# A two-block transformer in split fp32: first pair behind a norm in plain form, the two weight rings moved within a 256-byte line, and constant parts computed in other stages

## The chip, the cores and the metric

The kernel runs on one core of one Trainium2 chip. The metric is the device time of one execution in microseconds (us). The kernel before takes 1993.64 us, the median of three runs (1984.35 to 1995.71). Names of engines as in the profile: PE is TensorE's matmul, PEld its weight load, DVE is VectorE, ACT is ScalarE, POOL is GpSimd, SP is SyncE, whose queue issues the weight loads.

## The reference, cut to what matters

512 tokens of width 1024 go through two transformer layers, all in fp32. The second layer gets scales and shifts from a conditioning vector `c`. Cut to what the change touches:

```python
def second_block(x, c, w_ada, b_ada, ...):
    sh1, sc1, gt1, sh2, sc2, gt2, sh3, sc3, gt3 = split(silu(c) @ w_ada + b_ada, 9)
    u = rmsnorm_2(h, g_ff1) * (1 + sc1) + sh1
    h = h + 0.5 * gt1 * ((silu(u @ w1_gate) * (u @ w1_up)) @ w1_down)    # width 2816
    u = rmsnorm_2(h, g_mix) * (1 + sc2) + sh2
    ...                              # u @ w_in, differential attention, mLSTM
    h = h + gt2 * (merged @ w_out)
    u = rmsnorm_2(h, g_ff2) * (1 + sc3) + sh3
    h = h + 0.5 * gt3 * ((silu(u @ w2_gate) * (u @ w2_up)) @ w2_down)
    return rmsnorm_2(h, g_final)
```

Ahead of it, `first_block` does gated linear attention and windowed attention, and a feed-forward part of width 4096 with a squared relu; its output is normed once more and is then `h`.

## The kernel before, in words

**Precision.** Each fp32 operand is split into a high and a low part (`split`, L115 to L118: ACT writes the high part, DVE the difference). A product of two tiles is three matmuls: low by high, high by low, high by high (`mm3`, L124 to L126; `mm3k`, L130 to L132). Activations lie as 8 tiles of 128 features by 512 tokens, one per k.

**Plain and saving products.** `gemm` gives one output tile of 128 features by 512 tokens: 8 k times 3 = 24 matmuls of 512 columns. The wide matrices of the feed-forward parts go through `w_group` (L509) instead: a group makes four output tiles with the seven-product scheme of Strassen and Winograd, each product (`w_prod`, L498) 24 matmuls of 256 columns. It needs sums of the four weight blocks (L535, L543, L544, L554, on DVE), sums of the activation quarters (`w_sums`, L504 to L507), and DVE work behind the products (L527, L551, L558).

**Stages.** Attention of layer 1, its output product, feed-forward 1 (8 groups, each followed by 8 `down` tiles of the group before), the first feed-forward of layer 2 (`ffn_w(1, ...)`), the mixers, `merged`, `w_out2`, and the second feed-forward (`ffn_w(2, ...)`). Between the pieces of a group `fill` puts `down` tiles, `ada_step` (a piece of `silu(c) @ w_ada`, a 512 KB load and one DVE instruction of 1.28 us) and, in `ffn_w(1)`, `gate_weights`.

**A norm's border.** The scale of the norm comes only when all 8 tiles of the residual `res` stand. So four output tiles of the coming stage are computed ahead from the unscaled tiles (`pr` in the profile, 96 matmuls): the scale is multiplied in later (`ahead`), and the shift's part, weight times shift, is a constant per output feature. `prebias` (L415) computes that constant: load of the weight tile, one multiplication and seven multiply-adds on DVE (L423, L425, tile `pa`), a matmul of one column (L427), a copy (L428). Before, these calls stand in the loop over the 8 residual tiles just ahead of each border. Behind the border, `modulate` (L587) makes the scaled tiles one after the other, together with the sums that `w_group` wants, and ten groups follow.

**Order.** A list scheduler arranges the instructions of all engines when the kernel is built; each engine then works in order. Weight tiles go through rings of buffers: `wp` has three each of `raw`, `wh` and `wl`, the pool of a feed-forward stage (`hp`, tiles `s_...`) two of `wh` and `wl`. Before, a counter sends two of five splits to the second ring (L473, L474).

**Places in memory.** `shift` allocates a few bytes so that what follows starts elsewhere. As built before, the weight tiles of both rings start at byte 224 of a 256-byte line, and the activation tiles `uh`, `ul`, `vh`, `vl`, `hh`, `hl` at byte 160.

Of the kernel before, what the change touches and what calls it, by code (L numbers as in the profile page):

```python
# [18 lines left out]
P = 128  # L19
T = 512  # L20
# [34 lines left out]
class Kern:  # L55
    def __init__(self, tc, I, O, ctx):
        self.tc, self.nc, self.I, self.O = tc, tc.nc, I, O
        self.ctx = ctx
        ep = ctx.enter_context
        self.cst = ep(tc.tile_pool(name="cst", bufs=1))  # L60
        self.wp = ep(tc.tile_pool(name="wp", bufs=3))
        self.shift(self.wp, 128)
        self.sm = ep(tc.tile_pool(name="sm", bufs=2))
        self.wk = ep(tc.tile_pool(name="wk", bufs=2))
        self.dr = ep(tc.tile_pool(name="dr", bufs=1, space=bass.MemoryType.DRAM))
        self.roles = None
# [107 lines left out]

    def gemm(self, name, i, xh, xl, nk=KT, order=None, w=None):
        wh, wl = w or self.wtile(name, i, nk)
        ps = self.mmps()
        self.mm3(ps, wh, wl, xh, xl, nk, order)
        return ps
# [48 lines left out]
    def block1(self):  # L228
# [55 lines left out]
        def down(c, h, m2):  # L284
            w = self.w_split(self.w_load(I["w_ffd"][4 * c + m2]))
            wh, wl = (t.rearrange("p (a k m) -> p a k m", a=2, k=4) for t in w)
            for a in range(2):
                m = 2 * m2 + a
                ps = self.mmps()
                for k in range(4):  # L290
                    self.mm3k(ps, wh[:, a, k], wl[:, a, k], h[0][:, k // 2, k % 2], h[1][:, k // 2, k % 2], k, 3)
                V.tensor_tensor(out=res[:, m], in0=ps, in1=res[:, m], op=ALU.add)
                if c == NG_FF - 1:
                    if m == 0:
                        self.ada_gain(0)
                    self.boundary_tile(m)
                yield

        queue = iter(())
        for g in range(NG_FF):  # L300
            h = hid()

            def evict(c, a, b):
                s = slice(c * HT, (c + 1) * HT)
                for i, x in enumerate((a, b)):
                    r = self.wk.tile([P, T], F32, name="r1", tag="e1") if c and not i else x
                    rv = r.rearrange("p (a c) -> p a c", a=2)
                    V.scalar_tensor_tensor(out=rv, in0=x.rearrange("p (a c) -> p a c", a=2), scalar=0.0, in1=R[:, s].unsqueeze(1).to_broadcast([P, 2, HT]),
                                           op0=ALU.max, op1=ALU.mult)
                    act(out=r, in_=r, func=AF.Square)  # L310
                    self.split(h[0][:, :, i, s], h[1][:, :, i, s], rv)

            def fill(j):
                for _ in range(FILL_FF[g][j]):
                    next(queue)
                self.ada_step(j < 3)

            self.w_group(I["w_ffw"][g], (vh, vl), tt, ready, evict, fill, g == 0)
            assert next(queue, None) is None or g == 0
            queue = itertools.chain(*[down(g, h, m2) for m2 in range(KT // 2)])  # L320
# [6 lines left out]
    def ada_start(self, pool):  # L327
        nc = self.nc
        self.adp = pool
        if not hasattr(self, "mods"):  # L330
            self.mods = self.cst.tile([P, 72], F32, name="mods")
            self.sh, self.G = [None] * 3, [None] * 3
# [21 lines left out]
    def ada_gain(self, i):  # L354
# [3 lines left out]
        assert self.ada_i >= 24 * i + 16  # L358
        self.sh[i] = mod(3 * i)
        g = self.G[i] = c.tile([P, KT], F32, name=f"G{i}")  # L360
# [13 lines left out]
    def second_set(self):  # L374
        up = self.ue.enter_context(self.tc.tile_pool(name="up", bufs=1))
        self.shift(up, 64)
        return tuple(up.tile([P, KT, T], F32R, name=n) for n in ("vh", "vl"))


    def boundary_tile(self, m):  # L380
# [88 lines left out]

    def w_tile(self, tag, dt, own=None):  # L470

        if own is None:
            self.wn += tag == "wh"  # L473
            own = self.wn % 5 in (1, 3)  # L474
        small = self.raws if tag == "raw" else 2
# [8 lines left out]

    def w_split(self, raw):
        h, l = (self.w_tile(t, F32R).rearrange("p k m -> p (k m)")[:, :raw.shape[-1]] for t in ("wh", "wl"))
        self.split(h, l, raw)
# [21 lines left out]
    def w_group(self, src, u, tt, ready, evict, fill, early=False):  # L509
# [7 lines left out]
        A11, A21 = self.w_load(src[0], 0), self.w_load(src[1], 1)  # L517
        w = self.w_split(A11)
        self.w_prod(X, w, *blk(0, 0), first=True)
# [4 lines left out]
        def z(A12):  # L524
            w = self.w_split(A12)
            self.w_prod(Z, w, *blk(1, 0), first=True)
# [8 lines left out]
        V.tensor_tensor(out=S, in0=A11, in1=A21, op=ALU.add)  # L535
        w = self.w_split(S)
        A22 = self.w_load(src[2])
# [6 lines left out]
        V.tensor_tensor(out=A11, in0=A11, in1=A21, op=ALU.add)  # L544
        w = self.w_split(A11)
        self.w_prod(X, w, *sums(2))
        un = tmp("wu_", "wu", self.hp, 1)
        act(out=un, in_=X, func=AF.Copy)
        w = self.w_split(A22)
        self.w_prod(W, w, *sums(3))  # L550
# [4 lines left out]
        evict(0, p, un)  # L555
        w = self.w_split(A21)
# [3 lines left out]
        w = self.w_split(A12)  # L560
        self.w_prod(X, w, *blk(1, 1))
# [3 lines left out]
    def ffn_w(self, n, i, scale, pre, u, each, ada=False, final=False):  # L565
# [5 lines left out]
        with self.tc.tile_pool(name=f"hid_{n}", bufs=1) as hp:  # L571
# [5 lines left out]
            for j in range(2 * NPRE):  # L577
                wh, wl = self.wtile(wgu, j)
                ps.append(self.bank("pr"))
                self.mm3(ps[-1], wh, wl, *pre)  # L580
            hid = lambda: tuple(hp.tile([P, 2, T], F32R, name=t, tag=t, bufs=4) for t in ("hh", "hl"))
# [30 lines left out]
            def down(c, hs, m2):  # L612

                nk = 2 * len(hs)
                w = self.w_split(self.w_load(self.I[f"wdw{n}_{c}"][m2]))
                wh, wl = (t.rearrange("p (a k m) -> p a k m", a=2, k=nk) for t in w)
# [14 lines left out]
            for g in range(NG_W):  # L631
# [14 lines left out]
                def fill(j):  # L646
                    if g == 0 and j == 1:
                        ahead(1)
                        if len(rcol) > 1:
                            rp = self.bcast(rcol[1])  # L650
                            for k in range(KT):
                                V.scalar_tensor_tensor(out=res[:, k], in0=res[:, k], scalar=self.vec("final_norm_w")[:, k:k + 1], in1=rp, op0=ALU.mult, op1=ALU.mult)
# [7 lines left out]
                self.w_group(self.I[f"wgw{n}"][g], u, tt, ready, evict, fill, g == 0)  # L660
            for _ in queue:
# [8 lines left out]
            for c in range(2):  # L670
                cs = slice(c * HT, (c + 1) * HT)
                for m in range(KT):
                    if c == 0 and m % 2 == 0:
                        w = self.w_split(self.w_load(self.I[f"wdw{n}_{c_}"][m // 2]))
                        ws.append(tuple(t.rearrange("p (a k m) -> p a k m", a=2, k=4) for t in w))
# [9 lines left out]
    def block2(self):  # L685
# [6 lines left out]
        def each(m):  # L692
# [22 lines left out]
        for m in range(KT):  # L715
# [26 lines left out]
    def mix(self, scale, pre):  # L742
# [20 lines left out]
        with tc.tile_pool(name="g4", bufs=1) as g4:  # L763
# [985 lines left out]
def layout(inp):  # L1749
# [39 lines left out]
    for n in (1, 2):  # L1789
        gu = interleave(pack(a[f"w{n}_gate_2"][0]), pack(a[f"w{n}_up_2"][0]))  # L1790
        o[f"wgw{n}"] = blocks(gu[2 * NPRE:])
        o[f"wgu{n}"] = np.ascontiguousarray(gu[:2 * NPRE])
        w = a[f"w{n}_down_2"][0]
# [37 lines left out]
```

## Time and profile before

| | before |
|---|---|
| median of three runs | 1993.64 us |
| the profiled execution, its own time | 1992.08 us |
| its span, first to last instruction | 1990.3 us |
| mean granted TensorE clock | 0.985 |
| PE busy | 1925.4 us (97%), 10952 matmuls |
| DVE busy | 1511.2 us (76%) |
| ACT busy | 874.5 us (44%) |
| chain that ended last | PE 79%, DVE 14%, DMA 3%, ACT 2%, issue 2% |
| read from HBM | 225.74 MB |

A matmul's busy time runs from its start to its modelled end, and the next starts long before that end; so busy PE is not PE at its rate. The rate is the distance between starts. The rows below give windows of the whole kernel, and then single instructions with start and duration.

### The profile page before, as it was taken

How to read it: one execution, taken by the hardware profiler on the slowest of the kernel's cores; microseconds unless marked ns; L12 is line 12 of the kernel's file. 1: busy time of each engine (PE TensorE's matmuls, PEld its weight loads, DVE VectorE, ACT ScalarE, POOL GpSimd, SP SyncE). 2: the span in 40 equal slices, each digit the busy share in tenths (PEclk: the TensorE clock that was granted, in tenths of full speed). 3: DMA queues.
4: the chain of work that ended last, by engine and by line, in shares of the span. 5: the costliest groups of instructions: out<-in, count | busy, mean ns of one | idle time of the engine just before them, and what ended most of it. 6: DMA issues, size and time to landing. Idle time of an engine off the chain costs nothing.

```text
span 1990.3 us, 28105 instructions
## 1 busy us (share of the span) xinstructions
PE 1925.4 (97%) x10952; PEld 1601.7 (80%) x10952; DVE 1511.2 (76%) x2612; ACT 874.5 (44%) x1418; POOL 30.2 (2%) x47
## 2 busy tenths in 40 slices
PE   8999999999999799999999999999999998999997
PEld 5775689889887589999877877776678877999996
DVE  6687599778878998888887655676757878777776
ACT  4344555444434544444455444344442245444443
POOL 0000000000000000000000000111100000000000
PEclk9999999999999799999999999999999998999999
DMA  5220244444433244545342231323358722333321
GB/s 192 66 58 12 93 153 157 127 144 141 135 119 120 61 152 156 164 149 164 122 157 85 84 125 58 104 91 95 96 174 275 268 86 78 114 116 96 107 85 54
DMA packets 74335, 240.50 MB, mean 121 GB/s; under 512 B 8997, under 2 KB 12214, under 8 KB 74202
## 3 DMA queue, kind: packets, MB, share of 16 engines
q1 hardware_dynamic: 57274, 189.75, 29.8%
q10 hardware_dynamic: 16928, 48.96, 7.6%
q8 instruction: 86, 1.41, 0.3%
q14 instruction: 47, 0.39, 0.1%
HBM read 225.74 MB, written 8.41 MB: 118 GB/s over the span
## 4 chain that ended last, share of the span: by engine, by line
PE 79%; DVE 14%; DMA 3%; ACT 2%; issue 2%; DVEq 0%; SPq 0%; POOL 0%; ACTq 0%; POOLq 0%
PE x L498 13%; PE mm L130 9%; PE mm L131 9%; PE mm L132 9%; PE w L498 6%; PE mm L124 6%; PE mm L126 6%; PE mm L125 6%; PE z L498 3%; DVE wl L118 3%; PE po L1647 1%; DVE pa L425 1%; PE sw L1619 1%; DMA adaw<-in_w_ada 1%; DVE adaw L349 1%
## 5 line engine op out<-in xcount | busy, mean ns | idle before, releaser
L117 ACT ACTIVATE wh<-raw 128x1024 fp32r<-128x1024 f32 (+1 forms) x375 | 391.2, 1045 | 491.3 <-PE mm L132 217.1
L118 DVE TENSOR_TENSOR wl<-raw,wh 128x1024 fp32r<-128x1024 f32 (+1 forms) x375 | 451.5, 1207 | 105.5 <-ACT wh L117 104.5
L130 PE MATMUL mm<-hh,wl 128*128 128x512 f32 (+1 forms) x640 | 247.1, 386 | 4.2 <-DVE wl L118 2.0
L131 PE MATMUL mm<-hl,wh 128*128 128x512 f32 (+1 forms) x640 | 246.8, 386 | 0.1
L132 PE MATMUL mm<-hh,wh 128*128 128x512 f32 (+1 forms) x640 | 246.6, 385 | 0.0
L124 PE MATMUL mm<-uh,wl 128*128 128x512 f32 x560 | 226.8, 406 | 2.1 <-ACT uh L117 1.9
L126 PE MATMUL mm<-uh,wh 128*128 128x512 f32 x560 | 225.3, 402 | 0.0
L125 PE MATMUL mm<-ul,wh 128*128 128x512 f32 x560 | 224.6, 401 | 0.3 <-DVE ul L118 0.3
L130 PEld LDWEIGHTS mm<-hh,wl 128*128 128x128 f32 x640 | 120.9, 189 | 29.2 <-DVE res L623 2.3
L132 PEld LDWEIGHTS mm<-hh,wh 128*128 128x128 f32 x640 | 120.9, 189 | 25.8
L131 PEld LDWEIGHTS mm<-hl,wh 128*128 128x128 f32 x640 | 120.9, 189 | 23.8 <-DVE hl L118 0.5
L124 PEld LDWEIGHTS mm<-uh,wl 128*128 128x128 f32 x560 | 105.5, 189 | 36.6 <-issue 6.6
L498 PE MATMUL x<-uh,wl 128*128 128x256 f32 x448 | 125.9, 281 | 5.5 <-DVE sg L599 2.3
L498 PE MATMUL x<-vh,wl 128*128 128x256 f32 x448 | 126.6, 283 | 4.2 <-DVE wq__6292 L558 1.8
L498 PE MATMUL x<-vl,wh 128*128 128x256 f32 x448 | 125.8, 281 | 0.2 <-DVE vl L118 0.2
L498 PE MATMUL x<-vh,wh 128*128 128x256 f32 x448 | 125.7, 281 | 0.0
L126 PEld LDWEIGHTS mm<-uh,wh 128*128 128x128 f32 x560 | 105.8, 189 | 24.7 <-issue 2.3
L498 PE MATMUL x<-ul,wh 128*128 128x256 f32 x448 | 125.4, 280 | 0.1
L125 PEld LDWEIGHTS mm<-ul,wh 128*128 128x128 f32 x560 | 105.5, 188 | 24.8 <-issue 1.5
L498 PE MATMUL x<-uh,wh 128*128 128x256 f32 x448 | 124.9, 279 | 0.0
L349 DVE CUSTOM_DVE_ANT_0 adaw<-adaw,cb,c_vecs 128x1024 f32<-128x1024 f32 x72 | 91.4, 1278 | 18.2 <-DMA adaw<-in_w_ada 18.2
L623 DVE SCALAR_TENSOR_TENSOR res<-mm,gt,res 128x512 f32<-128x512 f32 x88 | 65.8, 748 | 48.6 <-PE mm L132 48.5
(936 smaller groups left out, 4284.1 us busy)
## 6 DMA issues: line engine op xcount, KB each, us to landing
raw<-in_wgw SPq DMA_DIRECT2D x80, 512.0 KB
adaw<-in_w_ada ACTq DMA_DIRECT2D x72, 512.0 KB
raw<-in_wdw SPq DMA_DIRECT2D x40, 512.0 KB
raw<-in_w_ffw SPq DMA_DIRECT2D x32, 512.0 KB
raw<-in_w_ffd SPq DMA_DIRECT2D x32, 512.0 KB
raw<-in_w_g SPq DMA_DIRECT2D x20, 512.0 KB
raw<-in_w_out SPq DMA_DIRECT2D x16, 512.0 KB
raw<-in_wgu SPq DMA_DIRECT2D x16, 512.0 KB
```

The costliest lines, as they stand in the source:

```text
L117: nc.scalar.activation(out=h, in_=src, func=AF.Copy)
L118: nc.vector.tensor_tensor(out=l, in0=src, in1=h.bitcast(F32), op=ALU.subtract)
L124: mm(ps, lhsT=wl[:, k], rhs=xh[:, k], start=(k == order[0]), stop=False)
L125: mm(ps, lhsT=wh[:, k], rhs=xl[:, k], start=False, stop=False)
L126: mm(ps, lhsT=wh[:, k], rhs=xh[:, k], start=False, stop=(k == order[-1]))
L130: mm(ps, lhsT=al, rhs=bh, start=(k == 0), stop=False)
L131: mm(ps, lhsT=ah, rhs=bl, start=False, stop=False)
L132: mm(ps, lhsT=ah, rhs=bh, start=False, stop=(k == last))
L349: ins = nc.vector.tensor_tensor_reduce(out=w, in0=w, in1=self.cb, scale=0.5, scalar=self.vec("b_ada_2", 72)[:, i:i + 1], op0=ALU.mult, op1 ...
L425: V.scalar_tensor_tensor(out=a, in0=raw[:, k], scalar=self.sh[i][:, k:k + 1], in1=a, op0=ALU.mult, op1=ALU.add)
L498: mm(o, lhsT=l[:, a, k], rhs=r(k), start=(first and a == 0 and k == 0 and j == 0), stop=(k == 3 and j == 2), skip_group_check=True)
L623: V.scalar_tensor_tensor(out=res[:, m], in0=ps, scalar=gt[:, m:m + 1], in1=res[:, m], op0=ALU.mult, op1=ALU.add)
```

## The change

- Behind both norms of `ffn_w`, the first group of four tiles is computed by four plain `gemm` calls in four different PSUM banks; nine groups follow in place of ten. The weights are stored accordingly.
- `prebias` for `ffn_w(1)` moves from the tail of feed-forward 1 into its groups 3 to 6; the four for `w_g` from the tail of `ffn_w(1)` into its passes 6 to 9; the four for `ffn_w(2)` from the `w_out2` loop into the last four passes of the loop over `merged`.
- `shift` ahead of `wp` disappears, and that of the later pool goes from 64 to 192 bytes. As built, the `wp` ring's weight tiles now start at byte 96 of a line; the second ring stays at 224 and the activation tiles stay at 160.
- Which ring a split uses is now written at each call: four of a group's seven products use the second ring, the other three and all `down` tiles use `wp`.

```diff
-        self.shift(self.wp, 128)
...
-                if c == NG_FF - 1:
-                    if m == 0:
-                        self.ada_gain(0)
                     self.boundary_tile(m)
...
+                if j == 3 and 3 <= g < 3 + 2 * NPRE:
+                    self.prebias("wgu1", g - 3, 0)
+            if g == 6:
+                self.ada_gain(0)
...
-        self.shift(up, 64)
+        self.shift(up, 192)
...
-        if m < 2 * NPRE:
-            self.prebias("wgu1", m, 0)
...
-    def w_split(self, raw):
-        h, l = (self.w_tile(t, F32R)...
+    def w_split(self, raw, own):
+        h, l = (self.w_tile(t, F32R, own)...
...
+                        if j == 2 and g >= 6:
+                            self.prebias("w_g", g - 6, 1)
+                if g:
+                    self.w_group(self.I[f"wgw{n}"][g - 1], u, tt, ready, evict, fill)
+                    continue
+                for t in range(2):
+                    pg, pu = (self.gemm(wgu, 2 * (NPRE + t) + j, *u, role=("z", "w", "x", "x")[2 * t + j]) for j in range(2))
+                    if t == 0:
+                        ahead(1)
+                        ready()
+                    r = self.wk.tile([P, T], F32, name="wr_", tag="e1")
+                    act(out=r, in_=pg, func=AF.Silu)
+                    V.tensor_tensor(out=r, in0=pu, in1=r, op=ALU.mult)
+                    self.split(h[0][:, t], h[1][:, t], r)
...
-            if m < 4:
-                self.prebias("w_g", m, 1)
...
-            if m < 2 * NPRE:
-                self.prebias("wgu2", m, 2)
...
+                    if m >= KT - 2 * NPRE:
+                        self.prebias("wgu2", m - KT + 2 * NPRE, 2)
...
-        o[f"wgw{n}"] = blocks(gu[2 * NPRE:])
+        o[f"wgw{n}"] = blocks(gu[2 * NPRE + 4:])
```

Line numbers of the changed kernel are lower by one to eight in this part (L498 becomes L493, L425 becomes L423). Three places of the built order follow.

PE, behind the border into `ffn_w(1)`, before; `z` and `w` are products of 256 columns, and `uh`, `ul` here hold the sums of activation quarters:

```order
L498 MATMUL z<-vh,wl 128x256
L498 MATMUL z<-vl,wh 128x256
L498 MATMUL z<-vh,wh 128x256
L498 MATMUL w<-uh,wl 128x256
L498 MATMUL w<-ul,wh 128x256
L498 MATMUL w<-uh,wh 128x256
```

The same place of the change; `z` and `w` are now banks of two plain tiles:

```order
L123 MATMUL z<-vh,wl 128x512
L124 MATMUL z<-vl,wh 128x512
L125 MATMUL z<-vh,wh 128x512
L123 MATMUL w<-vh,wl 128x512
L124 MATMUL w<-vl,wh 128x512
L125 MATMUL w<-vh,wh 128x512
```

Both tiles take the modulated tiles `vh`, `vl` alone, at full width; the sums are no longer read here, and the waits on them have moved to the next group.

DVE, tail of feed-forward 1, before (`ssq` is the norm's sum of squares, `ul` the low part of a tile computed ahead):

```order
L425 SCALAR_TENSOR_TENSOR pa<-raw,mods,pa 128x128 x4
L413 SCALAR_TENSOR_TENSOR ul<-res,G_5373,uh 128x512
L205 TENSOR_TENSOR ssq<-ssq,sq 128x512 x2
L425 SCALAR_TENSOR_TENSOR pa<-raw,mods,pa 128x128
L292 TENSOR_TENSOR res<-mm,res 128x512
L428 COPY pb<-at 128x1
```

The same tail of the change:

```order
L291 TENSOR_TENSOR res<-mm,res 128x512
L117 TENSOR_TENSOR wl<-raw,wh 128x1024
L411 SCALAR_TENSOR_TENSOR ul<-res,G_4627,uh 128x512
L204 TENSOR_TENSOR ssq<-ssq,sq 128x512 x2
L291 TENSOR_TENSOR res<-mm,res 128x512 x2
```

All `pa` instructions have left the tail. They stand, for instance, here in the change, on DVE in group 3 of feed-forward 1:

```order
L421 TENSOR_SCALAR pa<-raw,mods 128x128
L423 SCALAR_TENSOR_TENSOR pa<-raw,mods,pa 128x128
L117 TENSOR_TENSOR wl<-raw,wh 128x1024
L423 SCALAR_TENSOR_TENSOR pa<-raw,mods,pa 128x128 x2
L291 TENSOR_TENSOR res<-mm,res 128x512
L350 ISA adaw,mods<-adaw,cb,c_vecs 128x1024
```

The pieces of `pa` lie between splits and residual additions; the one-column matmul that reads `pa` stands a good part of a group later on PE.

## Rows read from the trace of the kernel before

**Rows 1.** Windows of the kernel: busy us and count by engine, clock, DMA share.

```profile
core 0: us, PE busy (x) PEld busy (x) DVE busy (x) ACT busy (x) POOL busy (x), PEclk, DMA share, GB/s
...
320.00:590.00 270.00, 270.00 (x1707) 242.96 (x1706) 213.89 (x268) 113.94 (x143) 0.00 (x0) 1.00 0.43 135
590.00:628.00 38.00, 34.08 (x138) 26.77 (x137) 30.49 (x64) 19.53 (x29) 0.00 (x0) 0.91 0.40 125
...
660.00:690.00 30.00, 20.10 (x93) 16.47 (x94) 28.34 (x47) 18.26 (x27) 0.00 (x0) 0.60 0.13 33
...
735.00:985.00 250.00, 250.00 (x1787) 229.79 (x1786) 211.63 (x258) 111.74 (x140) 0.00 (x0) 1.00 0.48 152
...
1640.00:1665.00 25.00, 16.62 (x78) 13.44 (x77) 20.87 (x33) 16.55 (x23) 0.00 (x0) 0.73 0.10 31
```

**Rows 2.** PE in order of time: tail of feed-forward 1.

```profile
618.10 0.38 PE L427 MATMUL at<-ones,pa 128*128 128x1 f32 x2 [1.78 <-DVE pa L425]
620.49 0.79 PE L130 MATMUL mm<-hh,wl 128*128 128x512 f32 x1 [2.01 <-DVE wl L118]
621.94 0.63 PE L130 MATMUL mm<-hh,wl 128*128 128x512 f32 x1
628.55 0.40 PE L124 MATMUL pr<-uh,wl 128*128 128x512 f32 x1
```

**Rows 3.** PE in order of time: behind the border into the first feed-forward.

```profile
651.37 1.10 PE L224 MATMUL at<-dg,ones 128*128 128x512 f32 x2
...
657.43 0.38 PE L498 MATMUL z<-vh,wl 128*128 128x256 f32 x1 [2.49 <-ACT vh L117]
...
681.63 0.41 PE L498 MATMUL x<-vh,wl 128*128 128x256 f32 x1
...
713.16 0.28 PE L498 MATMUL w<-uh,wl 128*128 128x256 f32 x1
```

**Rows 4.** DVE in order of time: first and last of the modulation behind each border.

```profile
653.13 1.41 DVE L587 SCALAR_TENSOR_TENSOR ut<-res,G,at 128x512 f32<-128x512 f32 x2
...
678.38 1.29 DVE L118 TENSOR_TENSOR vl<-ut,vh 128x512 fp32r<-128x512 f32 x2
...
1632.06 1.41 DVE L587 SCALAR_TENSOR_TENSOR ut<-res,G,at 128x512 f32<-128x512 f32 x2 [1.85 <-ACT R L433]
...
1659.13 1.29 DVE L118 TENSOR_TENSOR ul<-ut,uh 128x512 fp32r<-128x512 f32 x2
```

**Rows 5.** PE in order of time: one tile of 24, and the second feed-forward.

```profile
1614.19 0.40 PE L124 MATMUL mm<-uh,wl 128*128 128x512 f32 x1
...
1619.79 0.40 PE L124 MATMUL pr<-vh,wl 128*128 128x512 f32 x1
...
1691.94 0.28 PE L498 MATMUL w<-vh,wl 128*128 128x256 f32 x1
```

**Rows 6.** PE at both ends of the token-major products, and the count there.

```profile
1123.92 0.39 PE L130 MATMUL mm<-wh,ul 128*128 128x512 f32 x1
...
1145.68 0.39 PE L132 MATMUL mm<-wh,uh 128*128 128x512 f32 x1
...
1123.90:1145.85 21.95, 21.95 (x97) 17.84 (x95) 17.29 (x39) 7.69 (x9) 0.52 (x1) 1.00 0.26 75
```

**Rows 7.** Chain in order of time: start, us, what; two products of 24.

```profile
317.19 2.83 PE x L498 x24
...
742.81 2.73 PE x L498 x24
```

**Rows 8.** The tile of the constant parts, and who waited for it.

```profile
L425 DVE SCALAR_TENSOR_TENSOR pa<-raw,mods,pa x84: 340/348/355, 584.0 to 1596.9; 128x128 f32<-128x128 f32 x84
...
  PEld at L427: 4.5, 4
```

**Rows 9.** A pass of the loop over `merged`, as a window.

```profile
1546.00:1557.00 11.00, 11.00 (x49) 8.84 (x48) 8.37 (x13) 2.75 (x3) 0.00 (x0) 1.00 0.68 237
```

**Rows 10.** Split of a weight tile, from the page's costliest groups.

```profile
L118 DVE TENSOR_TENSOR wl<-raw,wh 128x1024 fp32r<-128x1024 f32 (+1 forms) x375 | 451.5, 1207 | 105.5 <-ACT wh L117 104.5
```

More of the change, by code (lines that the diff above doesn't have):

```diff
@@ L173, in atps, with gemm @@
         return self.bank("at")
-    def gemm(self, name, i, xh, xl, nk=KT, order=None, w=None):
+    def gemm(self, name, i, xh, xl, nk=KT, order=None, w=None, role="mm"):
         wh, wl = w or self.wtile(name, i, nk)
-        ps = self.mmps()
+        ps = self.bank(role)
         self.mm3(ps, wh, wl, xh, xl, nk, order)
@@ L284, in down @@
         def down(c, h, m2):
-            w = self.w_split(self.w_load(I["w_ffd"][4 * c + m2]))
+            w = self.w_split(self.w_load(I["w_ffd"][4 * c + m2]), False)
             wh, wl = (t.rearrange("p (a k m) -> p a k m", a=2, k=4) for t in w)
@@ L331, in ada_start @@
             self.mods = self.cst.tile([P, 72], F32, name="mods")
-            self.sh, self.G = [None] * 3, [None] * 3
+            self.sh, self.G = [self.mods[:, 24 * i:24 * i + 8] for i in range(3)], [None] * 3
             self.ada_i = 0
@@ L358, in ada_gain @@
         assert self.ada_i >= 24 * i + 16
-        self.sh[i] = mod(3 * i)
         g = self.G[i] = c.tile([P, KT], F32, name=f"G{i}")
@@ L468, in w_ready, with w_tile @@
         return ready, tt
[L470 to L474, printed above, removed]
+    def w_tile(self, tag, dt, own):
         small = self.raws if tag == "raw" else 2
@@ L483, in w_load @@
         return raw
-    def w_split(self, raw):
-        h, l = (self.w_tile(t, F32R).rearrange("p k m -> p (k m)")[:, :raw.shape[-1]] for t in ("wh", "wl"))
+    def w_split(self, raw, own):
+        h, l = (self.w_tile(t, F32R, own).rearrange("p k m -> p (k m)")[:, :raw.shape[-1]] for t in ("wh", "wl"))
         self.split(h, l, raw)
@@ L517, in w_group @@
         A11, A21 = self.w_load(src[0], 0), self.w_load(src[1], 1)
-        w = self.w_split(A11)
+        w = self.w_split(A11, True)
         self.w_prod(X, w, *blk(0, 0), first=True)
@@ L524, in z @@
         def z(A12):
-            w = self.w_split(A12)
+            w = self.w_split(A12, True)
             self.w_prod(Z, w, *blk(1, 0), first=True)
@@ L535, in w_group @@
         V.tensor_tensor(out=S, in0=A11, in1=A21, op=ALU.add)
-        w = self.w_split(S)
+        w = self.w_split(S, False)
         A22 = self.w_load(src[2])
@@ L544, in w_group @@
         V.tensor_tensor(out=A11, in0=A11, in1=A21, op=ALU.add)
-        w = self.w_split(A11)
+        w = self.w_split(A11, True)
         self.w_prod(X, w, *sums(2))
@@ L548, in w_group @@
         act(out=un, in_=X, func=AF.Copy)
-        w = self.w_split(A22)
+        w = self.w_split(A22, False)
         self.w_prod(W, w, *sums(3))
@@ L555, in w_group @@
         evict(0, p, un)
-        w = self.w_split(A21)
+        w = self.w_split(A21, True)
         self.w_prod(X, w, *sums(0))
@@ L559, in w_group @@
         fill(2)
-        w = self.w_split(A12)
+        w = self.w_split(A12, False)
         self.w_prod(X, w, *blk(1, 1))
@@ L577, in ffn_w @@
             for j in range(2 * NPRE):
-                wh, wl = self.wtile(wgu, j)
-                ps.append(self.bank("pr"))
-                self.mm3(ps[-1], wh, wl, *pre)
+                ps.append(self.gemm(wgu, j, *pre, role="pr"))
             hid = lambda: tuple(hp.tile([P, 2, T], F32R, name=t, tag=t, bufs=4) for t in ("hh", "hl"))
@@ L614, in down @@
                 nk = 2 * len(hs)
-                w = self.w_split(self.w_load(self.I[f"wdw{n}_{c}"][m2]))
+                w = self.w_split(self.w_load(self.I[f"wdw{n}_{c}"][m2]), False)
                 wh, wl = (t.rearrange("p (a k m) -> p a k m", a=2, k=nk) for t in w)
@@ L646, in fill @@
                 def fill(j):
[L647 to L652, printed above, removed]
                     for _ in range(FILL_W[g][j]):
@@ L658, in fill @@
                             self.gate_weights(g - 3)
-                self.w_group(self.I[f"wgw{n}"][g], u, tt, ready, evict, fill, g == 0)
+                        if j == 2 and g >= 6:
[12 more added lines that the diff above has]
+                    self.split(h[0][:, t], h[1][:, t], r)
+                if len(rcol) > 1:
+                    rp = self.bcast(rcol[1])
+                    for k in range(KT):
+                        V.scalar_tensor_tensor(out=res[:, k], in0=res[:, k], scalar=self.vec("final_norm_w")[:, k:k + 1], in1=rp, op0=ALU.mult, op1=ALU.mult)
+                for j in range(4):
+                    fill(j)
             for _ in queue:
@@ L673, in ffn_w @@
                     if c == 0 and m % 2 == 0:
-                        w = self.w_split(self.w_load(self.I[f"wdw{n}_{c_}"][m // 2]))
+                        w = self.w_split(self.w_load(self.I[f"wdw{n}_{c_}"][m // 2]), m < 4)
                         ws.append(tuple(t.rearrange("p (a k m) -> p a k m", a=2, k=4) for t in w))
@@ L1790, in layout @@
         gu = interleave(pack(a[f"w{n}_gate_2"][0]), pack(a[f"w{n}_up_2"][0]))
-        o[f"wgw{n}"] = blocks(gu[2 * NPRE:])
-        o[f"wgu{n}"] = np.ascontiguousarray(gu[:2 * NPRE])
+        o[f"wgw{n}"] = blocks(gu[2 * NPRE + 4:])
+        o[f"wgu{n}"] = np.ascontiguousarray(gu[:2 * NPRE + 4])
         w = a[f"w{n}_down_2"][0]
```

## The prediction

> **What bounds the kernel now.** I read the share of each engine on the chain first (in the table above: PE 79%, DVE 14%), then windows, then single instructions at the places where PE is not dense. In feed-forward 1 and in the body of the next feed-forward PE is busy without a break, while DVE is at 213.89 of 270 us and 211.63 of 250 us [rows 1]. There only PE's rate counts, and DVE has some 15 to 20% to spare. [...] Ahead of the first border, in 590 to 628, PE has 34.08 of 38 us at 0.91 [rows 1]. [...]
>
> **Part 1, the constants leave the tails.** In the tail of feed-forward 1 PE waits 1.78 us for `pa` and 2.01 us for a split that stands behind it on DVE; the clock then falls, a matmul takes 0.63 us in place of 0.40, and 24 matmuls need 628.55 - 620.49 = 8.06 us [rows 2]. At the dense rate (1614.19 to 1619.79, 5.60 us for 24, 0.2333 each [rows 5]) they would need 5.60. So 1.78 + 2.01 + 2.46 = 6.3 us go, if nothing is late in their place. What is late next is DVE's own list there: 30.49 us in this window [rows 1] less four constants of 2.4 us (below) is 20.9 us, against PE's 34.08; I expect PE to wait for it hardly at all. In the two other tails less is lost: all waits of the weight load for `pa` are 4.5 us in the whole kernel [rows 8], most of the first tail's among them; I take 2.
>
> The moved work is not free. Twelve constants bring twelve 512 KB loads on SP's queue, 84 `pa` multiply-adds of 0.348 us [rows 8], 2.4 us of DVE a constant as an upper bound, and a one-column matmul each. In feed-forward 1, 2.4 us fall on a group (168 + 96 of 1707 matmuls, 41.8 of the 270 us) that has 8.7 us of idle DVE [rows 1]: hidden, and the one-column matmul stands far behind on PE, so it waits for nothing. In `ffn_w(1)` the margin is 38 us of 250 [rows 1]. In the loop over `merged` it is thin: 8.37 us of DVE in a pass of 11 us, DMA at 0.68 [rows 9]; with 2.4 us more DVE reaches 10.8, and the load adds about a sixth to a pass's traffic. `ada_step` waits for loads there, and behind it on DVE stand the splits that PE wants. I charge 3 us, bounds 0 (all hidden) and 12 x 2.4 = 29 us (nothing hidden).
>
> **Part 2, the plain pair.** I compare from the first matmul computed ahead (`pr`) to the first `w` product of the next group, where the same output tiles and the eight two-k `down` tiles are done before and after.
>
> Before, the first border takes 713.16 - 628.55 = 84.6 us [rows 2, 3]. The broadcast of the scale comes at 651.37, 22.8 us in, and modulation starts at 653.13 and ends at 679.67, 26.5 us later, since DVE makes tiles and sums in turn [rows 3, 4]. PE takes three matmuls at a time (first after a 2.49 us wait), runs at the low clock (0.41 us for a product's matmul at 681.63, 0.28 later) [rows 3], and has four products left when the last tile stands.
>
> In the changed order the broadcast stands behind 73 of the 96 `pr` matmuls: 73 x 0.229 + 1 us of short sums = 17.7 us. DVE's chain up to it held nine instructions of the size of a split, 1.2 us [rows 10], and now holds four; 6 us earlier than 22.8 is 16.8, so PE's place decides. Modulation then starts at 17.7 + 1.8 (653.13 - 651.37 [rows 3, 4]) = 19.5 and needs again some 27 us: its instructions are the same. When the last pair of tiles stands, PE has done the earlier k of three of the four plain tiles and has 3 x 6 + 24 = 42 matmuls left: 9.6 us. Then 48 `down` matmuls, 11.0 us, and 24 of the next group's first product, 2.7 us [rows 7]. Sum 19.5 + 27 + 9.6 + 11.0 + 2.7 = 69.8 us, against 84.6: -14.8 us.
>
> The second border takes 1691.94 - 1619.79 = 72.2 us [rows 5], its modulation 1632.06 to 1660.42, 28.4 us [rows 4]. After the change the broadcast stands behind 30 `pr` matmuls, so modulation starts 9 us in; 9 + 27 + 9.6 + 11.0 + 2.7 = 59.3 us. PE's own work is 192 matmuls x 0.229 = 44.0, plus 1.5 for sums and broadcast, plus 13.7: 59.2 us. Both are equal, so this border turns into a bound by PE: -12.9 us. The three more microseconds of PE that plain form costs (96 x 0.229 = 22.0 against 168 x 0.1137 = 19.1) are in these sums.
>
> At the first border PE still waits 1 to 5 us for single tiles, and such waits brought the clock down in rows 2 and 3. I add 2 us for that; bounds 0 and 22 (half of the 192 plain matmuls at half rate, 96 x 0.229). Part 2 gives -25.7 us.
>
> **Part 3, the places of the rings.** With weights at byte 224 and streamed tiles at 160, the streamed address is 192 ahead of the weights modulo 256, and a 512-column matmul takes 0.2333 us [rows 5]. In the token-major products the roles change (weights 160, streamed 224, that is 64 ahead): 96 matmuls start from 1123.92 to 1145.68 (97 touch the window, one of them from before), 21.76 / 95 = 0.2290 us [rows 6]. The change brings the `wp` ring to 96 with streamed tiles at 160: 64 ahead. That distance, not the bytes themselves, decides is my reading; no row shows 96 with 160. Counted in the built program, 3990 such matmuls change, 192 of them the plain pairs (priced above). 2688 lie in dense stretches: 2688 x 0.0043 = 11.6 us. The other 1110 are in attention, where PE waits anyway; half counts, 2.4 us. The token-major products themselves become 192 ahead: 290 x 0.0043 = 1.2 us lost. Term -12.8 us, bounds +5 (distance decides nothing and the new place is somewhat worse) and -17.
>
> [...]
>
> [...]
>
> **Sum.** -6.3 - 2 + 3 - 25.7 - 12.8 = -43.8 us, from the profiled execution's 1992.08 us (span 1990.3) to 1948.3. The median is 1.6 us above that execution, which I leave out: 1948.5.
>
> **The rivals.** (a) The place in a line does nothing: part 3 is 0, 1961. [...] Chance 0.16.
>
> (b) The new mix of rings throws the second layer's products out of step, onto the rate 0.1179: 18 groups x 168 x 0.0042 = 12.7 us, 1961. For it: rows 7 show that the slow rate can last for a whole stage. Chance 0.10.
>
> (c) The border stays bound by DVE, and stop-and-go keeps the clock low: part 2 loses its upper bound of 22 us, 1970. For it: DVE is at 28.34 of 30 us there [rows 1]; against it, that the plain pair gives PE twelve matmuls a tile where it had three or six. Chance 0.10.
>
> (d) Slower: a constant's tile lands late while DVE, which works in order, stands at `pa`, with the splits of the running group behind it. In the tail one such stop cost 6.3 us with the clock [rows 2]; twelve in formerly dense stages cost 75 us: 2024. It decides from (1993.6 - 1948.5) / 12 = 3.8 us a constant. Against it: DVE's spare share in these stages [rows 1], and three `raw` buffers, so that a load runs while others are used. Chance 0.06.
>
> **How the numbers follow.** The forecast has 0.58, with its own range 1936 to 1962. Cases (a) to (c) all end below 1984, that is faster by over 0.5% (10 us, about what a measurement of this kernel tells from no change). Two of them together reach 1975 to 1983. So faster 0.88; the same 0.06, from the tops of (b) and (c) and a mild (d); slower 0.06, from (d). The range goes down to 1926, where part 3 gives 17, feed-forward 1 also gets the fast product rate (1344 x 0.0042 = 5.6) and the borders 6 us more, and up to 1978.
>
> **What would show it.** Tail: no `pa` in it, the first `pr` matmul 6 to 8 us earlier against the last product. Borders: 70 and 59 us by the same marks, granted clock near 1. Places: dense tiles of 24 at 5.50 us in place of 5.60, token-major matmuls at 0.233. Body groups: PE without breaks where constants now stand. Wrong would be 5.60 us a tile, a border over 78 or 68 us, or waits for `pa` in the groups.

## The result and the profile after

The changed kernel takes 1942.2 us (median of 4 runs, 1941.36 to 1944.1) against 1991.33 us before (also 4 runs, 1984.35 to 1995.71): a ratio of 0.9758, 95% interval 0.9726 to 0.9789, faster by 2.4%, which is 48 us. Forecast were 1948.5 us, range 1926 to 1978. Below, two profiled executions are compared, whose spans are 1990.3 and 1939.6 us, 50.7 us apart. PE's share of the chain went from 79% to 90%, DVE's from 14% to 7%.

Windows of the changed kernel, columns as in [rows 1]. The stretches are the body of feed-forward 1, its tail, the two parts of border 1 with waits, the body of the next feed-forward, the loop over `merged` and border 2.

```profile
320.00:583.00 263.00, 263.00 (x1709) 238.31 (x1708) 219.63 (x296) 113.20 (x141) 0.00 (x0) 1.00 0.47 144
583.00:613.00 30.00, 30.00 (x133) 24.62 (x132) 23.55 (x33) 18.27 (x26) 0.00 (x0) 1.00 0.37 104
640.00:657.00 17.00, 13.17 (x49) 8.30 (x48) 16.70 (x29) 9.08 (x14) 0.00 (x0) 1.00 0.06 16
657.00:675.00 18.00, 13.29 (x51) 10.36 (x52) 15.67 (x25) 10.36 (x16) 0.00 (x0) 0.91 0.28 85
705.00:954.00 249.00, 249.00 (x1806) 230.76 (x1806) 217.95 (x280) 111.59 (x138) 0.00 (x0) 1.00 0.51 159
1490.00:1582.00 92.00, 92.00 (x404) 74.78 (x403) 69.20 (x110) 29.54 (x37) 0.00 (x0) 1.00 0.69 232
1606.00:1645.00 39.00, 39.00 (x191) 32.61 (x190) 33.95 (x49) 20.99 (x30) 0.00 (x0) 1.00 0.22 66
```

The tail is dense at clock 1.00 (30.00 of 30 us; 34.08 of 38 at 0.91 before). DVE carries more in the bodies (219.63 of 263 us, 213.89 of 270 before) and PE doesn't stop for it. Of these stretches only border 1 still has gaps, with DVE at 16.70 of 17 us.

PE in order of time at the marks of [rows 2, 3, 5]: last product and first `pr` matmul; the two longest waits behind border 1; first `w` product of the next group; a tile of 24 and the second `pr`; the `w` product behind border 2.

```profile
582.64 0.28 PE L493 MATMUL x<-vh,wh 128*128 128x256 f32 x1
...
612.97 0.39 PE L123 MATMUL pr<-uh,wl 128*128 128x512 f32 x1
...
659.85 0.80 PE L123 MATMUL z<-vh,wl 128*128 128x512 f32 x1 [3.50 <-ACT vh L116]
667.46 0.50 PE L123 MATMUL x<-vh,wl 128*128 128x512 f32 x1 [1.86 <-DVE wl L117]
...
686.88 0.28 PE L493 MATMUL w<-uh,wl 128*128 128x256 f32 x1
...
1577.09 0.39 PE L123 MATMUL mm<-uh,wl 128*128 128x512 f32 x1
1582.59 0.39 PE L123 MATMUL pr<-vh,wl 128*128 128x512 f32 x1
...
1642.83 0.28 PE L493 MATMUL w<-vh,wl 128*128 128x256 f32 x1
```

Tail: 612.97 - 582.64 = 30.3 us. Before it was 628.55 - 589.63 = 38.9, where the last product's row is

```profile
589.63 0.28 PE L498 MATMUL x<-vh,wh 128*128 128x256 f32 x1
```

Border 1: 73.9 us (84.6). Border 2: 60.2 us (72.2). A tile of 24: 5.50 us (5.60).

DVE behind border 1 (answering [rows 4]), the first and last start of the 96 token-major products [rows 6], a merged product from the chain (24 matmuls in one row) [rows 7], and the tile of the constant parts [rows 8]:

```profile
633.79 1.41 DVE L580 SCALAR_TENSOR_TENSOR ut<-res,G,at 128x512 f32<-128x512 f32 x2
...
647.98 0.74 DVE L665 SCALAR_TENSOR_TENSOR res<-res,c_vecs,at 128x512 f32<-128x512 f32 x1
...
660.00 1.28 DVE L117 TENSOR_TENSOR vl<-ut,vh 128x512 fp32r<-128x512 f32 x2
...
666.19 1.21 DVE L117 TENSOR_TENSOR wl<-raw,wh 128x1024 fp32r<-128x1024 f32 x1
```

```profile
1091.44 0.39 PE L129 MATMUL mm<-wh,ul 128*128 128x512 f32 x1
...
1113.60 0.39 PE L131 MATMUL mm<-wh,uh 128*128 128x512 f32 x1
```

```profile
324.89 2.72 PE x L493 x24
```

```profile
L423 DVE SCALAR_TENSOR_TENSOR pa<-raw,mods,pa x84: 340/351/355, 398.2 to 1521.4; 128x128 f32<-128x128 f32 x84
...
  DMA raw<-in_wgu: 5.5, 5
```

The `pa` work now begins at 398.2 us. DVE stands 5.5 us in all for loads of `wgu` tiles, five times, and neither PE nor PEld is listed as waiting for `pa` any more. The 50.7 us, by the starts of first and last matmuls of the stages in both traces, are: ahead of feed-forward 1 0.6, its body 6.4, its tail 8.6, border 1 10.7, body 2.1, everything up to the second `pr` 8.8, border 2 11.9, the rest 1.6.

### The profile page after: what moved, and what is told of

Its sections match the earlier page's. It is cut to its first block, busy times and chain, and to the rows that moved or that the text cites. A ratio compares the mean times of both kernels' runs of the same rounds, so it can differ in the third digit from the quotient of the medians.

```text
span 1939.6 us, 27715 instructions
## 1 busy us (share of the span) xinstructions
PE 1896.3 (98%) x10808; PEld 1583.5 (82%) x10808; DVE 1491.1 (77%) x2592; ACT 866.5 (45%) x1406; POOL 29.9 (2%) x47
## 4 chain that ended last, share of the span: by engine, by line
PE 90%; DVE 7%; ACT 2%; DMA 1%; issue 1%; DVEq 0%; SPq 0%; ACTq 0%
PE x L493 14%; PE mm L131 11%; PE mm L130 11%; PE mm L129 11%; PE mm L123 6%; PE w L493 6%; PE mm L125 6%; PE mm L124 6%; PE z L493 3%; PE po L1652 1%; DVE wl L117 1%; PE sw L1624 1%; PE sc L1041 1%; PE pn L1049 1%; PE po L1178 1%
## 5 line engine op out<-in xcount | busy, mean ns | idle before, releaser
L116 ACT ACTIVATE wh<-raw 128x1024 fp32r<-128x1024 f32 (+1 forms) x371 | 386.3, 1044 | 434.3 <-PE mm L131 128.5
L117 DVE TENSOR_TENSOR wl<-raw,wh 128x1024 fp32r<-128x1024 f32 (+1 forms) x371 | 446.0, 1206 | 117.2 <-ACT wh L116 116.3
L129 PE MATMUL mm<-hh,wl 128*128 128x512 f32 (+1 forms) x640 | 241.6, 378 | 1.4 <-DVE res L688 1.3
L493 PE MATMUL x<-vh,wl 128*128 128x256 f32 x416 | 116.2, 279 | 0.5 <-DVE wq__6195 L553 0.3
L493 PE MATMUL x<-uh,wl 128*128 128x256 f32 x416 | 115.3, 277 | 1.0 <-DVE wl L117 1.0
L493 PE MATMUL x<-vl,wh 128*128 128x256 f32 x416 | 115.5, 278 | 0.0
L493 PE MATMUL x<-vh,wh 128*128 128x256 f32 x416 | 115.1, 277 | 0.0
L493 PE MATMUL x<-ul,wh 128*128 128x256 f32 x416 | 115.0, 276 | 0.0
L493 PE MATMUL x<-uh,wh 128*128 128x256 f32 x416 | 115.0, 276 | 0.0
```

The costliest lines, as they stand in the source:

```text
L116: nc.scalar.activation(out=h, in_=src, func=AF.Copy)
L117: nc.vector.tensor_tensor(out=l, in0=src, in1=h.bitcast(F32), op=ALU.subtract)
L129: mm(ps, lhsT=al, rhs=bh, start=(k == 0), stop=False)
L493: mm(o, lhsT=l[:, a, k], rhs=r(k), start=(first and a == 0 and k == 0 and j == 0), stop=(k == 3 and j == 2), skip_group_check=True)
```

## The experiments

Each ratio is to the kernel before, run beside it on the same chip, and is compared with 0.9758 for the change; a step of 0.001 is 2 us. Spans, each of one profiled execution, are set against 1939.6. They are less sure: in two profiles of the kernel before, at equal code, feed-forward 1 starts at 279.3 and at 281.5 us.

**Old places.** One shift back in each of two pools.

```
+        self.shift(self.wp, 128)
-        self.shift(up, 192)
+        self.shift(up, 64)
```

> The changed kernel with both weight rings at byte 224 again (streamed tiles 192 ahead of the weights); all else as changed. Theory of the prediction (the distance sets the rate of 512-column matmuls): dense tiles of 24 at 5.60 us instead of 5.50, and 11.6 + 2.4 - 1.2 = 12.8 us are lost, about 1955. Second theory, from the trace of the changed kernel (the slow rate of 256-column products, 0.1178, hangs on the old places too): products of feed-forward 1 go back to 2.83 us each as well, some 6 us more, about 1961. Rival (the place does nothing and something else made the tiles faster): tiles stay at 5.50 us, time stays at 1942.

1957.99 us, ratio 0.9818 (0.979 to 0.9846), span 1953.6: 14.0 us lost in the spans, 12 by the ratios. PE, the last tile of 24 ahead of the second border:

```profile
1588.85 0.39 PE L124 MATMUL mm<-uh,wl 128*128 128x512 f32 x1
...
1594.45 0.39 PE L124 MATMUL pr<-vh,wl 128*128 128x512 f32 x1
```

```profile
444.47 2.72 PE w L494 x24
```

5.60 us again. The first theory holds (12.8 forecast). The second falls: 39 of the 47 merged products of feed-forward 1 take 2.72 or 2.73 in this execution (last row, from the chain), at the same places at which they took 2.83 before.

**Places alone.**

```
-        self.shift(self.wp, 128)
-        self.shift(up, 64)
+        self.shift(up, 192)
```

> The kernel before with the places of the rings alone changed (wp ring at 96, own ring at 224), so that the counter still chooses the ring: 3249 of the 512-column matmuls get weights at 96 (64 ahead), 705 keep 224 (192 ahead). If the distance sets the rate, both rates stand beside each other in one kernel: down tiles from the wp ring at 5.50 us for 24, those from the own ring at 5.60; time about 1992 - 10.5 = 1981, or about 1976 if the 256-column products of feed-forward 1 also become fast (2.72 us a product). If the place does nothing: 5.60 everywhere and 1992.

1987.23 us, ratio 0.9977 (0.9959 to 0.9995): only some 5 us. PE and chain: two runs of 36 matmuls of 512 columns, the first with weights from the `wp` ring, the second from the own ring (each ends where the next product starts), then two products.

```profile
368.31 0.39 PE L129 MATMUL mm<-hh,wl 128*128 128x512 f32 x1
...
376.56 0.28 PE L497 MATMUL x<-vh,wl 128*128 128x256 f32 x1
...
409.61 0.39 PE L129 MATMUL mm<-hh,wl 128*128 128x512 f32 x1
...
418.00 0.28 PE L497 MATMUL x<-vh,wl 128*128 128x256 f32 x1
```

```profile
440.28 2.83 PE x L497 x24
...
448.76 2.72 PE x L497 x24
```

8.25 us against 8.39, 0.2292 against 0.2331 in one stage: the place decides. Part of what is missing against the expectation is that products switch between two rates: by the distance between starts, the 256-column matmuls of the two feed-forwards of the second layer average 115.2 ns here and 113.7 before, 4.9 us over some 3200 of them.

**The counter chooses the ring**, in the changed kernel:

```
+        if tag != "raw":
+            self.wn += tag == "wh"
+            own = self.wn % 5 in (1, 3)
```

> The changed kernel with the counter choosing the weight ring again instead of the roles (the raw tiles' ring as changed). 705 of the 512-column matmuls fall back to weights at 224 and 0.2332 us: 705 x 0.0043 = 3.0 us, about 1945. Second theory, from the run with the places alone (changing between the two distances also throws the 256-column products onto the slower step, 115.4 instead of 113.8 ns on the mean): 4560 x 0.0016 = 7 us more, about 1952.

1954.21 us, ratio 0.9814 (0.9792 to 0.9836): the second theory. 20 of 47 merged products in the chain of feed-forward 1 take 2.83 or more (6 of 47 after the change, at 2.82 or 2.83). So giving the `down` weights to one ring was worth about as much as the new places, and much of either gain hangs on the other: in the kernel before, without the roles, the places gave 5 us, and taking back either alone from the changed kernel costs 11 to 14.

**Other distances.** The `wp` ring 64 or 192 bytes further, `up` back by as much.

```
+        self.wp.tile([P, 16], F32, name="shift", bufs=1)    # 48 for the second
-        self.shift(up, 192)
+        self.shift(up, 128)                                 # left out for the second
```

> The changed kernel with the wp ring at byte 160, the place of the streamed tiles: 4338 of the 512-column matmuls read both operands from the same place modulo 256 bytes (distance 0). If the distance sets the rate, this one gets a rate of its own, different from 0.229 (64) and 0.233 (192); which one no run shows yet, I guess 0.233 and 1942 + 13 = 1955. If only the byte of the weights mattered (224 bad, others good) the rate stays at 0.229 and the time at 1942.

> The changed kernel with the wp ring at byte 32: 4038 of the 512-column matmuls at distance 128. In the run with the places alone 72 matmuls with weights at 96 and streamed tiles at 224 took 0.2323 us, as 72 with 224 and 96 did before the change; if the distance sets the rate, all dense tiles take 0.2323 and the time is 1942 + 3800 x 0.003 = about 1953. If only the byte 224 was bad: 0.229 and 1942.

1956.99 us, ratio 0.9829 (0.9804 to 0.9853), and 1967.88, 0.9886 (0.9863 to 0.991). PE's tile of 24 and one product of the chain, distance 0:

```profile
1585.66 0.39 PE L124 MATMUL mm<-uh,wl 128*128 128x512 f32 x1
...
1591.10 0.39 PE L124 MATMUL pr<-vh,wl 128*128 128x512 f32 x1
```

```profile
442.76 2.88 PE w L494 x24
```

and distance 128:

```profile
1596.43 0.40 PE L124 MATMUL mm<-uh,wl 128*128 128x512 f32 x1
...
1602.03 0.40 PE L124 MATMUL pr<-vh,wl 128*128 128x512 f32 x1
```

```profile
445.64 2.85 PE w L493 x24
```

Tiles of 24 take 5.44, 5.50, 5.60, 5.60 us at distances 0, 64, 128, 192. Distance 0 is best for 512 columns and worst for 256 (2.88; 119.8 ns a matmul for the products with weights from the `wp` ring), and loses by the products. The products from the other ring, whose place did not change, slow down as well: 117.5 ns with `wp` at distance 0 and 116.7 at 128, against 113.9 after the change. The guess of 1955 for it was near for a wrong reason, and the time for 128 was missed by 15 us: both expectations left the products out.

**Constants back in the tails.** `ada_gain(0)`, which stood in the first tail too, goes back with them.

```
-                if j == 3 and 3 <= g < 3 + 2 * NPRE:
-                    self.prebias("wgu1", g - 3, 0)
+        if m < 2 * NPRE:
+            self.prebias("wgu1", m, 0)          # in boundary_tile; the other two likewise
```

> The changed kernel with the constant parts computed in the three tails again. By the prediction's terms 6.3 + 2 us come back and the 3 us charged for the moved constants go: 1942 + 5.3 = about 1947, and the tail of feed-forward 1 (last product to first pr matmul, 30.3 us after the change, 38.9 before) is 6 to 8 us longer with a wait for pa in it. If the moved constants cost nothing where they stand now: 1950. Rival (the moved constants cost as much as the tails gain): 1942, with the body of feed-forward 1 shorter by what the tail loses.

1952.15 us, ratio 0.9788 (0.9764 to 0.9812), span 1949.5: 9.9 us lost in the spans, 6 by the ratios, whose intervals overlap. The trace places the loss. PE in the tail of feed-forward 1 (last product 581.17):

```profile
601.45 0.38 PE L424 MATMUL at<-ones,pa 128*128 128x1 f32 x2 [0.53 <-DVE pa L422]
608.37 0.50 PE L129 MATMUL mm<-hh,wl 128*128 128x512 f32 x1 [0.69 <-DVE res L291]
617.75 0.47 PE L123 MATMUL pr<-uh,wl 128*128 128x512 f32 x1 [3.36 <-DVE wl L117]
```

The tail takes 36.6 us, 6.3 more. The three waits shown are 4.6 us of it, 3.36 of them for a weight split that DVE reaches late, with the constants in its list. The stretch from the end of the next feed-forward's products to the second `pr` takes 4.3 us more, though the kernel of the next experiment, which keeps the constants moved, has 2.2 of that too. The body of feed-forward 1, without its four constants, is 0.7 us shorter (303.2 for 303.9); that is no more than this body differs between profiles with the constants in it (303.8 to 305.2).

**Blocks again for the first pair.** The branch for `g == 0` goes, `w_group` gets group 0.

```
-                if g:
-                    self.w_group(self.I[f"wgw{n}"][g - 1], u, tt, ready, evict, fill)
-                    continue
+                self.w_group(self.I[f"wgw{n}"][g], u, tt, ready, evict, fill, g == 0)
```

> The changed kernel with the first pair behind each norm in block form again. By the prediction's sum 25.7 us come back: about 1968. By the marks of the two traces (first pr matmul to first w product of the next group: 84.6 to 73.9 us and 72.2 to 60.2 us) 10.7 + 11.9 = 22.6: about 1965; borders again near 84 and 72 us less what the rings give (about 1 us each). Rival (the plain form gains nothing by itself, the shorter borders come from the lighter DVE list and the rings): 1942 to 1946.

1967.38 us, ratio 0.9872 (0.9839 to 0.9906), span 1965.1. PE at the marks of both borders, and then a window behind border 1:

```profile
611.77 0.39 PE L123 MATMUL pr<-uh,wl 128*128 128x512 f32 x1
...
697.38 0.28 PE L493 MATMUL w<-uh,wl 128*128 128x256 f32 x1
...
1596.25 0.39 PE L123 MATMUL pr<-vh,wl 128*128 128x512 f32 x1
...
1668.48 0.28 PE L493 MATMUL w<-vh,wl 128*128 128x256 f32 x1
```

```profile
640.00:657.00 17.00, 7.64 (x21) 4.91 (x21) 16.79 (x30) 10.15 (x16) 0.00 (x0) 0.58 0.00 0
```

85.6 and 72.2 us: the plain pair is worth 11.7 + 12.0 = 23.7 at equal rings and constants. The rival is out. In blocks PE starts on some 20 matmuls of 256 columns in this window, at a granted clock of 0.58, against some 50 of 512 columns at 1.00 in the same window after the change; DVE is full in both (16.79 and 16.70 of 17 us). So the pair gives PE more to do while DVE makes the tiles, and the clock stays up. How much of the 23.7 us is the clock alone, these runs don't separate.

**Border 1: whose time is it?** In the changed kernel eight multiplications of `res` (L665) stand inside the modulation. First they are queued on DVE behind the first pair's product.

```
+                        with self.tc.issue_after(mul.ins):
                             rp = self.bcast(rcol[1])
```

> The changed kernel with the broadcast and the eight multiplications of res by the final norm issued on DVE behind the first pair's product instead of inside the modulation behind border 1. They take 8 x 0.66 = 5.3 us of DVE there, and PE waits 7.9 us in all in that stretch. If DVE's list sets that border: 73.9 to 68.6 us and about 1937, with the wait before the last tiles (3.50 us) gone. Rival: they now stand between the plain tiles and the first down tiles, which wait for res and for hl; PE waits there instead and the time stays within 2 us of 1942.

1943.47 us, ratio 0.976 (0.9737 to 0.9782): the time is the rival's. The border shrinks to 683.07 - 612.92 = 70.15 us, and PE waits at its end and behind it instead:

```profile
678.83 0.50 PE L129 MATMUL mm<-hh,wl 128*128 128x512 f32 x1 [1.44 <-DVE wl L117]
...
689.42 0.39 PE L493 MATMUL x<-uh,wl 128*128 128x256 f32 x1 [2.07 <-DVE wl L117]
```

But these waits are for weight splits, not for `res` and `hl` as the rival had it. Then, besides, three calls of `ada_step` leave the first group for later ones.

```
-                        self.ada_step(j in (1, 2) or j == 3 and g % 2 == 0)
+                        self.ada_step(g > 0 and (j in (1, 2) or j == 3))
```

> The run with the scaling later, and besides the three steps of the table for the next block (load of 512 KB and 1.28 us of DVE each) that stand in the first group behind border 1 go to later groups, where DVE has 31 us to spare of 249. In the run with the scaling later PE waited 1.44 and 2.07 us for weight splits at the end of this border, with DVE full (14.78 of 15 us in 675 to 690). If DVE's total work sets that border, 3.84 us less of it takes these waits away: 73.9 to about 70 us, and 1938 to 1940. Rival (the splits are late for another reason, their loads or the ring): 1942 to 1944 as in the run with the scaling later.

1943.73 us, ratio 0.9756 (0.9728 to 0.9785). The border shrinks to 70.0 us (685.56 - 615.55), 3.9 less than after the change, and PE pays it back behind it:

```profile
685.56 0.28 PE L493 MATMUL w<-uh,wl 128*128 128x256 f32 x1
...
690.01 0.39 PE L493 MATMUL w<-uh,wl 128*128 128x256 f32 x1 [1.46 <-ACT wq__6186 L536]
703.02 0.39 PE L493 MATMUL x<-vh,wl 128*128 128x256 f32 x1 [1.81 <-DVE wl L117]
```

The expectation of 1938 to 1940 fell. PE now waits for the split of a weight tile and for a copy out of the product's bank (`wq`) that stands between splits on ACT. The chain that ended last passes there, from 682.8 to 699.5 us, through DVE (residual additions, splits, sums of weight blocks), ACT's splits and then 3.67 us of a load of the next weights. That names several resources; which of them holds the border these runs don't settle.

**The multiplications off DVE**, on ScalarE and GpSimd.

```
-                        V.scalar_tensor_tensor(out=res[:, k], in0=res[:, k], scalar=self.vec("final_norm_w")[:, k:k + 1], in1=rp, op0=ALU.mult, op1=ALU.mult)
+                        act(out=res[:, k], in_=res[:, k], func=AF.Copy, scale=self.vec("final_norm_w")[:, k:k + 1])
+                        nc.gpsimd.tensor_tensor(out=res[:, k], in0=res[:, k], in1=R2, op=ALU.mult)
```

> The changed kernel with the eight multiplications of res by the final norm taken off DVE: ScalarE multiplies by the norm's weight (0.63 us each, as its copies with a scale), GpSimd by the broadcast scale (1.3 us each, as its products of 128x512 in the attention), together 8 x 1.3 = 10.4 us on an engine that is idle there. Moving the same work later on DVE left the time where it was (the run with the scaling later), which says that DVE's total work sets border 1. If so, 5.3 us less on DVE gives about 1937. Rival (PE is bound there by the order of the modulation and by late weight splits, not by DVE's total): within 2 us of 1942.

1956.61 us, ratio 0.9828 (0.9808 to 0.9847): some 14 us slower than the change. GpSimd, then DVE at the same time:

```profile
643.57 3.49 POOL L668 TENSOR_TENSOR res<-res,R 128x512 f32<-128x512 f32 x2 [535.80 <-ACT R L665]
```

```profile
645.84 1.50 DVE L499 TENSOR_TENSOR hl<-ut 128x256 f32<-128x256 f32 x1
647.27 0.41 DVE L500 TENSOR_TENSOR hl<-ut 128x256 f32<-128x256 f32 x1
647.60 3.43 DVE L117 TENSOR_TENSOR vl<-ut,vh 128x512 fp32r<-128x512 f32 x2
```

A DVE sum that takes 0.41 us takes 1.50 while GpSimd multiplies, and ends 0.28 us after GpSimd's second product (643.57 + 3.49 = 647.06). A pair of splits takes 3.43 instead of 1.28 (at 660.00 after the change). The border grew to 695.33 - 614.70 = 80.6 us, 6.7 more, and the stretch behind it, up to the second `pr`, by 6.3 us. Both expectations fell. Nor does the run answer the question that it was made for: the eight products left DVE, but other instructions of DVE became longer beside them (0.41 to 1.50 us, 1.28 to 3.43 us).

**Which of the two steps a product takes.** Both rings at 96, by the shift ahead of the own ring in either layer:

```
-            self.shift(hp, 64)
+            self.shift(hp, 192)
```

> The changed kernel with the own ring at byte 96 too, so that all 4560 of the 256-column products read weights 64 behind the streamed tiles. Theory: at distance 192 a 256-column product has two steps (113.3 and 117.8 ns) and keeps the one it is in, while at distance 64 it always falls to 113.3; then no product of 24 takes 2.83 us any more in the bodies, the mean goes from 113.8 to 113.4 and the time falls by 1 to 2 us, 1940 to 1941. Rival (the step does not hang on the distance): as many slow products as in the changed kernel, 1942.

and the kernel before once more, unedited.

> The kernel before once more, unchanged, for a second profile of it. In the first, every product of 256 columns in the body of feed-forward 1 took the slow step (2.83 us for 24), while in the run with the old places it took the fast one at the same places. If the step is a state that an execution falls into and keeps, this execution may show 2.72 us there, or a mixture, and its span moves by up to 5.6 us against 1990.3; if something in the program fixes it, 2.83 us again throughout.

Both at 96: 1954.29 us, ratio 0.9808 (0.9786 to 0.9829); the theory is refuted. Products of 2.83 and of 2.72 stand in one stage, 23 and 23 of the 47 merged ones in feed-forward 1, none of them at distance 192:

```profile
343.88 2.83 PE x L493 x24
```

```profile
444.34 2.72 PE w L493 x24
```

The kernel before again: 1993.43 us, span 1991.7, and

```profile
446.41 2.72 PE w L498 x24
```

All 45 merged products of feed-forward 1 are fast here (2.72 or 2.73), and all 45 were slow in the first profile (2.83 or 2.84), at equal code. Its body is 4.9 us shorter (305.4 for 310.3); everything else together took 6.3 us more. How often an execution of this kernel takes the one step or the other, two profiles don't tell.

## Why the prediction was right, step by step

**The places** (term -12.8, measured by the run with the old places -14.0 in the spans, -12 by the ratios). The reading that the distance decides, not the bytes, is confirmed: the token-major products, whose weights stayed at byte 160 while their streamed tiles went from 224 to 96, slowed from 0.2290 to (1113.60 - 1091.44) / 95 = 0.2333 us as forecast, the rate of weights at 224 with streamed tiles at 160, which is the same distance of 192. Rival (a) is out: at equal clock 1.00 a tile takes 5.44 to 5.60 us by the distance. Why, no run shows.

**The plain pair** (term -25.7, measured against blocks -23.7 at the two borders, -25.5 in the whole spans and -23 by the ratios, and -22.6 by the marks of before and after). Border 2 came as worked out: 60.2 for 59.3, bound by PE. Border 1 was put at 69.8 and took 73.9. Modulation started 20.8 us in for 19.5; it took 27.5 us for 27 (633.79 to 661.28); and one wait was not in the sum, the fourth plain tile's weight split, which stands behind the modulation on DVE: 1.86 us at 667.46. The 2 us for clock dips were mostly not needed: from 659.85 on, six matmuls start 0.43 us apart, and then 0.23 again.

**The constants** (term -5.3, measured -9.9 in the spans, -6 by the ratios). That the first tail gave 6.3 us to a tenth is luck: the forecast had 2.46 of them from the clock, but with the constants back the clock stays at 1.00 up to the first `pr` and falls to 0.50 only behind it (618.4 to 628.4; 0.91 on the mean from 617.8 to 692.7), and the loss is in other waits. The charge of 3 us for the moved work looks too high: the four in feed-forward 1 cost at most about 0.7, and in 1490 to 1582, where the loop over `merged` runs with its four, PE is busy 92.00 of 92 us. Rival (d) is out: DVE does stand for loads, 5.5 us in all, but no stop of several microseconds for each constant reaches PE in these stretches.

**The 256-column products** (no term in the sum). Here the account is weakest. Rival (b) and the low end of the range rest on the two rates of [rows 7], 2.83 / 24 = 0.1179 and 2.73 / 24 = 0.1137 us, and no run shows what chooses between them, or that it is a matter of step. The forecast looked for a change in the second layer; what differs is feed-forward 1, 117.3 to 114.0 ns over some 1310 matmuls, 4.3 us, which stood only in the lower end of the range. And the repeated run says that this need not be the change's: the first profiled execution before had taken the slow step in all merged products of that stage, the second one the fast step. Rival (b) did not come, though both rates stand in one stage in other runs: with the counter 20 of the 47 merged products of feed-forward 1 take 2.83 us or more, with both rings at 96 23 take 2.83 and 23 take 2.72. In five profiles with the places of the change (its own, the constants back, the blocks, the scaling later and on GpSimd) the means of the three feed-forward bodies lay between 113.3 and 114.2 ns for either ring. Why this mixture holds the fast step is open.

Undoing the places, the constants and the pair, one at a time, costs 14.0 + 9.9 + 25.5 = 49.4 of the 50.7 us in the spans, but 12 + 6 + 23 = 41 of 48 by the ratios; and undoing the roles of the rings, which the forecast priced only as a part of the places, costs another 11 to 12. So the parts are not independent, and that the spans add up is in part luck. Of rival (c) little is left: border 1 took 4 us more than forecast, not 22, and taking work off DVE there moved PE's waits but did not shorten the kernel.

The forecast lay 6 us too high, well inside its range. The 4.3 us of feed-forward 1's products would be most of that, and so would what the constants gave beyond their term in the spans; the runs don't tell which it is. Its low end, 1926, does not follow from the three reasons given for it: they take 4.2 + 5.6 + 6 us off 1948.5, which is 1932.7.

## What to carry to other kernels

Look at the addresses of stationary and streamed operands modulo 256 bytes when dense matmuls run a few per cent slow (here 5.60 us for 24 in place of 5.50 or 5.44); change the place and who uses it together (the places alone gave 5 us here), and measure the shapes apart, since distance 0 was the best here for 512 columns (5.44 us a tile) and the worst for 256 (2.88 us a product). Work that is independent of the running stage belongs where PE is dense and DVE has slack, even if it costs as much engine time there (here the tail of feed-forward 1 took 6.3 us less without its four constants, and the body with them at most about 0.7 more). A term of a per cent or less that rests on one profiled execution should be read from a second one first.

## What was not expected of the hardware

- With its operands 64 or 192 bytes apart modulo 256, a 256-column matmul took one of two steps in nearly all merged products of feed-forward 1, 113.3 or 117.8 ns (2.72 or 2.83 us for 24), and kept one for up to the whole stage (45 of 45 merged products slow, then 0 of 45, in two executions of the kernel before).
- In the body of feed-forward 1 a 512-column matmul took 227.5, 228.8, 232.7 and 233.2 ns with its operands 0, 64, 128 and 192 bytes apart modulo 256 (the runs with distance 0, the change, distance 128, the old places).
- Beside GpSimd products of 128x512, in the run with the scaling on GpSimd, DVE's sum `hl<-ut` at L499 took 1.50 us both times at border 1 (0.41 to 0.42 after the change), and each time ended 0.28 us after a GpSimd product. Why, no run shows.
